# A hybrid decoder step on one core: the first loads regrouped, half of the first row scaling on GpSimd, and the first transposes woven into the first product

## The chip, the cores and the metric

The kernel runs on one core of one Trainium2 chip. The metric is device time in microseconds; the median of the runs counts. Engines are named as in the profile: PE (TensorE matmul), PEld (its weight load), DVE (VectorE), ACT (ScalarE), POOL (GpSimd) and SP (SyncE, which here only issues transfers).

## The reference, cut to what matters

One inference step of one decoder layer over 512 prompt rows and 32 sample rows of 1024 numbers each. The part that the change touches is the very beginning: the row normalisation of x and the first columns of the input projection.

```python
h = x * rsqrt(mean(x * x, axis=-1) + EPS) * norm_mix_pre     # 544 rows of 1024
proj = h @ w_in                                              # 1024 x 4608, cut into x_r | q | k | v | g
# attention bias: rel_bias[bucket(distance)], a table of 32 x 8
# then: causal conv and RG-LRU, windowed attention, gates, w_out, RMSNorm,
# ConvFFN (w_up 1024 x 8192, depthwise conv, gelu(gate) * value, w_down), RMSNorm
```

## The kernel before, in words

All products are made from float32 numbers that are split into a high part (rounded to the fast matmul type) and a low part (the rest): a product of a weight tile and an activation tile is three matmuls, high x high, high x low and low x high. Activations are kept with features on partitions (`h`, tiles hH and hL, eight of each for the eight 128-wide blocks k of the 1024 features), rows along the free dimension in two halves: half 0 is rows 0 to 255, half 1 the other 288.

The weights come 128 output columns at a time, 512 KB each: `wload` (L254) issues the load on SP into one of five `raw` buffers; `wsplit_hi` (L277) makes the two high halves on ACT and `wsplit_lo` (L282) the two low halves on DVE. `order` lists the column tiles as they are used; the first is called w0 below, the next w1, and so on. `mmhalf` (L165 is the matmul inside) issues the 24 matmuls of one column tile and one half; `step` gives them a PSUM buffer, and its tick then records the vector work that is due.

PE's, DVE's and ACT's instructions are kept in the order in which the code records them. POOL's and SP's order is made by a scheduler from the dependences it sees, so it need not be the order of the lines.

The start goes as follows. SP issues four loads of 256 KB for the first 256 rows (`xload(0)`, `xload(1)`; each row tile in two column halves z), a small one for the first norm weights, w0 and w1, then the other rows (`xload(2)` to `xload(4)`) and w2 to w4. POOL's own queue carries five small loads: the table `c_ohp` (L377), `rel_bias` into `relx` (L375) and three groups of norm weights into `rows_a` (L379); behind them stand, from a later line, a memset of the tile `lt` (L535), four loads of `rel_bias` into `rel` (L538), and sixteen small copies from `rel` to `lt` (L559). PE runs 18 warming matmuls on constants.

`xsquares` (L407 on ACT for the left column half, L409 on DVE for the right) sums the squares of a row tile; `xrstd` adds the two sums and makes the reciprocal root (a square root on ACT, then a reciprocal and one refining step on DVE). `xscale` multiplies the four half tiles: one on ACT, behind the two high splits of w0, and three on DVE. Then PE transposes the eight blocks (`ps_ta`, L448, two transposes of 128 x 128 for each), and `hsplit` makes hH on ACT (L433) and hL on DVE (L177 with tile hL) from each block. The first product (column tile w0, half 0, PSUM tile `pmin`) comes behind all sixteen transposes, in the order high x high, low weight x high, high x low, eight matmuls each. The next product (w1, half 0) follows, then a small product `ps_ohp` of `relx` and `ohp`, then w2.

Of the kernel before, what the change touches and what calls it, by code (L numbers as in the profile page):

```python
# [11 lines left out]
F32 = mybir.dt.float32  # L12
F32R = mybir.dt.float32r
AF = mybir.ActivationFunctionType
ALU = mybir.AluOpType
AX = mybir.AxisListType

P = 128
D = 1024
KD = D // P  # L20
# [9 lines left out]
NH = 8  # L30
NKV = 2
HD = 128
WIN = 128
NBK = 32
# [4 lines left out]
EPS = 1e-6  # L39
# [84 lines left out]
def hawk_step(ctx, tc, I, O):  # L124
    nc = tc.nc
    act, dve, pool, pe = nc.scalar, nc.vector, nc.gpsimd, nc.tensor
# [13 lines left out]
    cp = mixer.enter_context(tc.tile_pool(name="mixer_const", bufs=1))  # L140
    mixer.enter_context(tc.manual_schedule(engines={act.engine, dve.engine}))

    def S(name, dt=F32):
        return sp.tile([P, SLOT], dt, tag="s", name=name)

    def T(name, dt=F32):
        return tp.tile([P, FLAT + 4], dt, tag="t", name=name)
# [4 lines left out]
    def PM(name):  # L152
        return psm.tile([P, 512], F32, tag="mm", name=name)

    def PX(name):
        return psx.tile([P, 512], F32, tag="aux", name=name)
# [4 lines left out]
    def f32(ap):  # L161
        return ap.bitcast(F32)

    def mm(out, l, r, start, stop):
        pe.matmul(out, l, r, start=start, stop=stop)  # L165
# [4 lines left out]
    def mul(out, a, b):  # L170
        dve.tensor_tensor(out=out, in0=a, in1=b, op=ALU.mult)

    def add(out, a, b):
        dve.tensor_tensor(out=out, in0=a, in1=b, op=ALU.add)  # L174

    def stt(out, a, s_, b, op0, op1):
        dve.scalar_tensor_tensor(out=out, in0=a, scalar=s_, in1=b, op0=op0, op1=op1)  # L177
# [9 lines left out]
    def sides():  # L187
        for e in sorted((e for e in side if e[0] <= now[0]), key=lambda e: e[:2]):
            try:
                e[0] = now[0] + (next(e[2]) or 1)  # L190
            except StopIteration:
                side.remove(e)

    def tick(target=0, dt=1):
        now[0] += dt
        todo = late[:]
        late.clear()
        split = [wsplit_hi(u) for u in wclaim(target)]
        sides()
        for f in todo:  # L200
            f()
        for u in split:
            wsplit_lo(*u)
        for f in last:
            f()
        last.clear()
# [6 lines left out]
    ident = keep.tile([P, P], F32, name="ident")  # L213
# [9 lines left out]
    def wsrc(key):  # L223
        kind = key[0]
        if kind in ("wr", "wi"):
            return I["lru_" + kind][0, 4 * key[1]:4 * key[1] + 4].rearrange("n c d -> c n d")
        w = {"in": w_in, "lo": I["w_lru_o"][0], "ao": I["w_attn_o"][0], "out": I["w_out"][0]}[kind]
        c = key[-1]
        return w[:, c * P:(c + 1) * P].rearrange("(k p) n -> p k n", p=P)

    qkv_order = (16, 18, 8, 9, 10, 11, 17, 19, 12, 13, 14, 15)
    order = [("in", c) for c in qkv_order]
# [6 lines left out]
    wpos = {k: i for i, k in enumerate(order)}  # L239
    in_slots = {("out", c) for c in range(3, 8)} | {("in", c) for c in qkv_order[3:FIRST]}  # L240
    wraw, wunits, wnext = {}, {}, [0]

    def wname(i):
        return "_".join(str(z) for z in order[i])

    def wload(i):
        key = order[i]
        raw = wraw[i] = rp.tile([P, KD, P], F32, tag="raw", name="raw_" + wname(i))
        if key[0] == "wg":
            for z, nme in enumerate(("lru_wr", "lru_wi")):  # L250
                nc.sync.dma_start(out=raw[:, 4 * z:4 * z + 4, :],
                                  in_=I[nme][0, 4 * key[1]:4 * key[1] + 4].rearrange("n c d -> c n d"))
        else:
            nc.sync.dma_start(out=raw, in_=wsrc(key))  # L254
# [26 lines left out]
    def wsplit_lo(raw, hl, eng=None):  # L281
        (eng or dve).tensor_tensor(out=hl[1], in0=raw, in1=f32(hl[0]), op=ALU.subtract)  # L282

    def upto(key, a, look):
        return 2 * (wpos[key] + look) + a + 1
# [28 lines left out]

    def mmhalf(ps, key, X, a, ks=range(KD)):
        n = X.half[a][1] - X.half[a][0]
        if key == order[0] and a == 0:

            for j, (i0, i1) in enumerate(((0, 0), (1, 0), (0, 1))):
                for k in ks:  # L320
                    mm(ps[:, :n], wunits[2 * wpos[key] + k // 4][i0][:, k % 4, :], X.get(k, a, i1),
                       j == 0 and k == 0, j == 2 and k == KD - 1)
            return
        for k in ks:
            wh, wl = (wunits[2 * wpos[key] + k // 4][j][:, k % 4, :] for j in range(2))
            xh, xl = X.get(k, a, 0), X.get(k, a, 1)
            mm(ps[:, :n], wh, xh, k == 0, False)
            mm(ps[:, :n], wh, xl, False, False)
            mm(ps[:, :n], wl, xh, False, k == KD - 1)

    def step(key, X, a, done, target=None, look=2, quick=False):


        ps = PM("pm" + "_".join(str(z) for z in key) + f"_{a}")
        if quick:
            mmhalf(ps, key, X, a, range(4))
            now[0] += 0.5
            sides()
            mmhalf(ps, key, X, a, range(4, 8))
            done(a, ps)  # L340
        else:
            mmhalf(ps, key, X, a)
        tick(upto(key, a, look) if target is None else target, 0.5 if quick else 1)
        if not quick:
            late.append(lambda: done(a, ps))
# [6 lines left out]
    rows_a = cp.tile([32, P], F32, name="rows_a")  # L352
    warm = keep.tile([P, 1], F32, name="warm")
    act.activation(warm, epst, AF.Sqrt)
    xt = {}

    def xload(i):
        t0, n, src = TOK[i]
        for z in range(2):
            xt[i, z] = S(f"x{i}_{z}")  # L360
            nc.sync.dma_start(out=xt[i, z][:n, 0:512], in_=src[:, 512 * z:512 * z + 512])

    xload(0)
    xload(1)
    nc.sync.dma_start(out=rows_a[0:8, :], in_=I["norm_mix_pre"].rearrange("o (k p) -> (o k) p", p=P))
# [2 lines left out]
    xload(2)  # L368
    xload(3)
    xload(4)  # L370
    for i in (2, 3, 4):
        wload(i)
    relx = cp.tile([NBK + 1, NH], F32, name="relx")
    pool.memset(relx, 1.0)
    pool.dma_start(out=relx[0:NBK, :], in_=I["rel_bias"])  # L375
    ohp = T("ohp")[:NBK + 1, 0:3 * WIN]
    pool.dma_start(out=ohp, in_=I["c_ohp"])  # L377
    for r, nme in ((8, "norm_mix_post"), (16, "norm_ffn_pre"), (24, "norm_ffn_post")):
        pool.dma_start(out=rows_a[r:r + 8, :], in_=I[nme].rearrange("o (k p) -> (o k) p", p=P))  # L379
    pv = keep.tile([P, 96], F32, name="pv")  # L380

    pw = PX("ps_warm")
    ps0 = PX("ps_rows_a0")
# [5 lines left out]
    def newton_rstd(r, v, s_, sq):  # L389

        act.activation(s_, sq, AF.Sqrt, scale=1.0 / D, bias=epst)
        dve.tensor_scalar(v, sq, 1.0 / D, EPS, ALU.mult, ALU.add)
        dve.reciprocal(r, s_)
        mul(s_, r, r)
        stt(s_, s_, -0.5, v, ALU.mult, ALU.mult)
        stt(r, s_, 1.5, r, ALU.add, ALU.mult)

    h = Full("h")
    for k in range(KD):
        h.alloc(k)  # L400
    ss = cp.tile([P, 4, 5], F32, name="ss")
    dve.memset(ss, 1.0)

    def xsquares(i):
        n = TOK[i][1]
        jk, jv = T(f"jk{i}"), T(f"jv{i}")
        act.activation(jk[:n, 0:512], xt[i, 0][:n, 0:512], AF.Square, accum_out=ss[:n, 0, i:i + 1])  # L407
        xb = xt[i, 1][:n, 0:512]
        dve.scalar_tensor_tensor(out=jv[:n, 0:512], in0=xb, scalar=1.0, in1=xb, op0=ALU.mult, op1=ALU.mult,  # L409
                                 accum_out=ss[:n, 1, i:i + 1])  # L410

    def xrstd(lo, hi):
        c = slice(lo, hi)
        add(ss[:, 0, c], ss[:, 0, c], ss[:, 1, c])
        newton_rstd(ss[:, 1, c], ss[:, 3, c], ss[:, 2, c], ss[:, 0, c])

    def xscale(i, engines):
        n = TOK[i][1]
        r = ss[:n, 1, i:i + 1]
        for z in range(2):  # L420
            x_ = xt[i, z][:n, 0:512]
            if engines[z] == "a":
                act.activation(x_, x_, AF.Copy, scale=r)
            else:
                dve.tensor_scalar(x_, x_, r, None, ALU.mult)

    def xtile(i, k):
        n = TOK[i][1]
        return xt[i, k // 4][:n, (k % 4) * P:(k % 4 + 1) * P]

    def hsplit(k, a, ps):
        g = pv[:, G_PRE + k:G_PRE + k + 1]
        act.activation(h.get(k, a, 0), ps, AF.Copy, scale=g)  # L433
        stt(h.get(k, a, 1), ps, g, f32(h.get(k, a, 0)), ALU.mult, ALU.subtract)

    xsquares(0)
    xsquares(1)
    xrstd(0, 2)
    split = [wsplit_hi(u) for u in wclaim(2)]
    xscale(0, "av")  # L440
    xscale(1, "vv")
    dve.tensor_copy(pv[:, 0:8], ps0[:, 0:8])
    for u in split:
        wsplit_lo(*u)
    for k in range(KD):
        ps = (PM if k in (5, 6) else PX)(f"ps_ta{k}")
        for i in range(2):
            pe.transpose(ps[:, i * P:(i + 1) * P], xtile(i, k), ident)  # L448
        hsplit(k, 0, ps[:, :256])

    def norm_b():
        last.extend(lambda i=i: xsquares(i) for i in (2, 3, 4))
# [1182 lines left out]
    for i, x in enumerate(plan):  # L1635
# [7 lines left out]
        else:  # L1643
            _, q, c, a = x
# [113 lines left out]
    for i in range(2):  # L1758
        for kk in range(2):
            ps = tokens(i, kk)  # L1760
# [13 lines left out]
    r = rstd(1)  # L1774
# [36 lines left out]
```

## Time and profile before

| | |
|---|---|
| runs | 1006.45, 1008.0 and 1010.39 us |
| median | 1008.0 us |
| the profiled execution | span 1006.6 us (from its first to its last instruction; no other time is given for it) |
| granted TensorE clock over the span | 0.996 of full |
| busy: PE, DVE, ACT, POOL | 98%, 73%, 58%, 15% of the span |

The profile is of one execution. All times inside it are counted from the start of its span. A row of the timeline gives start, duration, engine, line, operation, output and inputs, a count where rows were merged, and in brackets how long the engine had been idle and what ended that. A row of the windows gives, for a stretch of time, the busy time of each engine, the granted clock, the busy share of the transfer engines and what they moved.

### The profile page before, as it was taken

The numbers are of one execution on the slowest core, as the hardware profiler recorded it, in microseconds if no ns is written. First come the engines' busy times: TensorE is split into PE (matmuls) and PEld (weight loads), VectorE is DVE, ScalarE is ACT, GpSimd is POOL, SyncE is SP. The second block draws the span as 40 slices with busy tenths as digits, with TensorE's granted clock in tenths as the row PEclk, the third lists the DMA queues.
The fourth block names the chain that finished last, engine by engine and source line by source line (L and its number), as shares of the span: only waits on it lengthen the run. The fifth ranks groups of instructions, "written<-read, shape, count | busy, mean of one in ns | idle before, by whom it ended". The sixth has DMA issues, their size and how long they took to land.

```text
span 1006.6 us, 20151 instructions
## 1 busy us (share of the span) xinstructions
PE 991.0 (98%) x7819; PEld 980.2 (97%) x7819; DVE 731.3 (73%) x1552; ACT 579.9 (58%) x1421; POOL 150.5 (15%) x270
## 2 busy tenths in 40 slices
PE   7999999999999999999999999999999999999997
PEld 7999999999999999999999999999999999999995
DVE  6476688545935655489777788888888888878865
ACT  6444454468458534556776656565656555555652
POOL 3131010001404432120001111111111101110003
PEclk9999999999999999999999999999999999999999
DMA  7743222323322344417245858586867676776612
GB/s 209 231 145 97 63 80 85 110 88 90 97 84 85 105 137 133 120 53 222 71 111 127 193 123 192 125 191 126 189 134 181 145 170 153 162 169 157 215 45 90
DMA packets 207687, 133.40 MB, mean 133 GB/s; under 512 B 6546, under 2 KB 194306, under 8 KB 207560
## 3 DMA queue, kind: packets, MB, share of 16 engines
q1 hardware_dynamic: 197944, 112.20, 39.2%
q0 software_dynamic: 9600, 17.90, 11.2%
q10 hardware_dynamic: 48, 2.03, 0.5%
q8 instruction: 61, 1.00, 0.4%
q14 instruction: 34, 0.28, 0.1%
HBM read 111.82 MB, written 9.14 MB: 120 GB/s over the span
## 4 chain that ended last, share of the span: by engine, by line
PE 93%; DVE 2%; DMA 2%; ACT 1%; issue 0%; SPq 0%; DVEq 0%
PE pmin L165 22%; PE pmdn L165 17%; PE pux L1396 15%; PE puy L1396 7%; PE pq L1396 6%; PE pmout L165 5%; PE pmao L165 5%; PE pmlo L165 4%; PE puz L1396 4%; PE pg L165 1%; PE psc L165 1%; PE ptok L165 1%; PE pvp L165 1%; DMA raw_up_s<-in_w_up_dram 1%; DMA raw_in<-in_w_in_dram 1%; PE pt L701 1%
## 5 line engine op out<-in xcount | busy, mean ns | idle before, releaser
L165 PE MATMUL pmin<-hH,wh_in 128*128 128x256 f32 (+1 forms) x576 | 167.1, 292 | 0.0
L165 PE MATMUL pmin<-hH,wl_in 128*128 128x256 f32 (+1 forms) x576 | 164.8, 288 | 0.0
L165 PE MATMUL pmin<-hL,wh_in 128*128 128x256 f32 (+1 forms) x576 | 164.7, 288 | 0.0
L165 PE MATMUL pmdn<-fH,wh_dn 128*128 128x256 f32 (+1 forms) x448 | 129.3, 289 | 0.2 <-DVE ft L174 0.2
L165 PE MATMUL pmdn<-fH,wl_dn 128*128 128x256 f32 (+1 forms) x448 | 129.3, 289 | 0.2 <-DVE wl_dn L168 0.2
L165 PE MATMUL pmdn<-fL,wh_dn 128*128 128x256 f32 (+1 forms) x448 | 129.2, 288 | 0.0
L177 DVE SCALAR_TENSOR_TENSOR uc<-u,fv,uc 128x560 f32<-128x560 f32 x128 | 101.9, 796 | 13.3 <-ACT uc L1427 13.2
L165 PEld LDWEIGHTS pmin<-hH,wh_in 128*128 128x128 f32 x576 | 108.3, 189 | 1.5 <-issue 0.6
L165 PEld LDWEIGHTS pmin<-hL,wh_in 128*128 128x128 f32 x576 | 108.2, 189 | 0.0
L165 PEld LDWEIGHTS pmin<-hH,wl_in 128*128 128x128 f32 x576 | 107.9, 188 | 0.0
L165 PEld LDWEIGHTS pmdn<-fH,wh_dn 128*128 128x128 f32 x448 | 84.4, 188 | 0.6 <-issue 0.6
L165 PEld LDWEIGHTS pmdn<-fH,wl_dn 128*128 128x128 f32 x448 | 84.5, 189 | 0.4 <-DVE wl_dn L168 0.4
L165 PEld LDWEIGHTS pmdn<-fL,wh_dn 128*128 128x128 f32 x448 | 84.3, 188 | 0.0
L1522 ACT COPY u<-pux 128x272 f32<-128x272 f32 x52 | 20.1, 386 | 85.9 <-PE pux L1396 85.9
L168 DVE TENSOR_TENSOR u<-puy,u 128x240 f32<-128x240 f32 (+2 forms) x78 | 24.6, 344 | 50.1 <-PE puy L1396 32.5
L174 DVE TENSOR_TENSOR ft<-ft,pmdn 128x256 f32<-128x256 f32 (+1 forms) x104 | 45.2, 435 | 16.2 <-PE pmdn L165 15.9
L277 ACT ACTIVATE wh_in<-raw_in 128x512 fp32r<-128x512 f32 x72 | 44.2, 628 | 20.8 <-PE pmin L165 10.4
L282 DVE TENSOR_TENSOR wl_in<-raw_in,wh_in 128x512 fp32r<-128x512 f32 x72 | 48.2, 683 | 1.6 <-ACT wh_in L277 1.5
L1427 ACT ACTIVATE uc<-u,fv 128x560 f32<-128x560 f32 x64 | 48.2, 754 | 0.0
L664 ACT ACTIVATE s<-s,st 128x256 f32<-128x256 f32 (+1 forms) x32 | 15.2, 475 | 50.7 <-DVE st L661 43.3
L168 DVE TENSOR_TENSOR wl_dn<-raw_dn,wh_dn 128x512 fp32r<-128x512 f32 x56 | 38.3, 685 | 0.0
L1322 POOL DMA_DIRECT2D raw_up_s<-raw_up_s x26 | 22.7, 872 | 101.7 <-issue 5.0
(758 smaller groups left out, 3406.3 us busy)
## 6 DMA issues: line engine op xcount, KB each, us to landing
raw_in<-in_w_in_dram SPq DMA_DIRECT2D x36, 512.0 KB
raw_dn<-in_w_down_dram SPq DMA_DIRECT2D x56, 256.0 KB
raw_up_s<-in_w_up_dram SPq DMA_DIRECT2D x26, 512.0 KB
raw_up_s<-raw_up_s POOLq DMA_DIRECT2D x26, 256.0 KB, 5.8
raw_ao<-in_w_attn_o_dram SPq DMA_DIRECT2D x8, 512.0 KB
raw_lo<-in_w_lru_o_dram SPq DMA_DIRECT2D x8, 512.0 KB
raw_out<-in_w_out_dram SPq DMA_DIRECT2D x8, 512.0 KB
x1d<-x SPq DMA_DIRECT2D x8, 272.0 KB
```

Of the source, the lines that this page charges most:

```text
L165: pe.matmul(out, l, r, start=start, stop=stop)
L168: dve.tensor_tensor(out=out, in0=a, in1=b, op=ALU.subtract)
L174: dve.tensor_tensor(out=out, in0=a, in1=b, op=ALU.add)
L177: dve.scalar_tensor_tensor(out=out, in0=a, scalar=s_, in1=b, op0=op0, op1=op1)
L277: act.activation(hl[0], raw, AF.Copy)
L282: (eng or dve).tensor_tensor(out=hl[1], in0=raw, in1=f32(hl[0]), op=ALU.subtract)
L664: act.activation(s3[:, j, :], s3[:, j, :], AF.Exp, bias=ng[:, j:j + 1], accum_out=sm[:, j:j + 1])
L701: pe.transpose(pt[:, (2 * ch + j) * P:(2 * ch + j + 1) * P], s3[:, j, ch * P:(ch + 1) * P], ident)
L1322: pool.dma_start(out=w["p4"], in_=w["p2"], accum_op=ALU.add)
L1396: pe.matmul(ps[:, :HN], w, x, start=start and k == 0 and i == 0, stop=stop and k == 3 and i == 2, skip_group_check=True)
L1427: act.activation(yt[j][:, 0:FLATU], u[:, 0:FLATU], AF.Copy, scale=fv[:, j:j + 1])
L1522: act.copy(e[nm_], z)
```

## The change

- The five small loads leave POOL's queue. They are issued by SP, behind the row tiles and w2 and ahead of w3 and w4.
- The sum of squares is finished otherwise: POOL makes `vsum` from ACT's sums, DVE adds its own sums to that in one instruction, and the square root reads the result.
- Of the four half tiles that are scaled, DVE takes three and POOL one (row tile 1, right half). ACT takes none.
- The two low halves of w0 are made on POOL.
- The first product gets its PSUM buffer (`pm_first`) before the transposes, and its matmuls stand between them: high x high two blocks behind the transposes, high x low three blocks behind, and the eight low weight x high ones last.

In the built program everything else stands as before on each engine. On POOL the scheduler places the new instructions behind what was there: memset `relx`, memset `lt`, the four loads of `rel`, the sixteen copies to `lt`, then `vsum`, the first low half of w0, the scaling, the second low half of w0.

```diff
@@ mmhalf, step @@
-        if key == order[0] and a == 0:
-
-            for j, (i0, i1) in enumerate(((0, 0), (1, 0), (0, 1))):
-                for k in ks:
-                    mm(ps[:, :n], wunits[2 * wpos[key] + k // 4][i0][:, k % 4, :], X.get(k, a, i1),
-                       j == 0 and k == 0, j == 2 and k == KD - 1)
-            return
...
-        ps = PM("pm" + "_".join(str(z) for z in key) + f"_{a}")
-        if quick:
+        first_ = key == order[0] and a == 0
+        ps = first_ps if first_ else PM("pm" + "_".join(str(z) for z in key) + f"_{a}")
+        if first_:
+            pass
+        elif quick:
@@ loads @@
-    for i in (2, 3, 4):
-        wload(i)
-    relx = cp.tile([NBK + 1, NH], F32, name="relx")
-    pool.memset(relx, 1.0)
-    pool.dma_start(out=relx[0:NBK, :], in_=I["rel_bias"])
-    ohp = T("ohp")[:NBK + 1, 0:3 * WIN]
-    pool.dma_start(out=ohp, in_=I["c_ohp"])
+    wload(2)
+    nc.sync.dma_start(out=relx[0:NBK, :], in_=I["rel_bias"])
+    nc.sync.dma_start(out=ohp, in_=I["c_ohp"])
     for r, nme in ((8, "norm_mix_post"), (16, "norm_ffn_pre"), (24, "norm_ffn_post")):
-        pool.dma_start(out=rows_a[r:r + 8, :], in_=I[nme].rearrange("o (k p) -> (o k) p", p=P))
+        nc.sync.dma_start(out=rows_a[r:r + 8, :], in_=I[nme].rearrange("o (k p) -> (o k) p", p=P))
+    wload(3)
+    wload(4)
@@ start @@
-    xrstd(0, 2)
+    pool.tensor_scalar(vsum, ss[:, 0, 0:2], 1.0 / D, EPS, ALU.mult, ALU.add)
+    r_, s_, v_ = (ss[:, z, 0:2] for z in (1, 2, 3))
+    stt(v_, ss[:, 1, 0:2], 1.0 / D, vsum, ALU.mult, ALU.add)
+    act.activation(s_, v_, AF.Sqrt)
+    dve.reciprocal(r_, s_)
+    mul(s_, r_, r_)
+    stt(s_, s_, -0.5, v_, ALU.mult, ALU.mult)
+    stt(r_, s_, 1.5, r_, ALU.add, ALU.mult)
     split = [wsplit_hi(u) for u in wclaim(2)]
-    xscale(0, "av")
-    xscale(1, "vv")
-    dve.tensor_copy(pv[:, 0:8], ps0[:, 0:8])
+
+    def scale0(eng, i, z):
+        eng.tensor_scalar(xt[i, z][:, 0:512], xt[i, z][:, 0:512], ss[:, 1, i:i + 1], None, ALU.mult)
+
+    scale0(dve, 0, 0)
+    scale0(pool, 1, 1)
+    scale0(dve, 1, 0)
+    scale0(dve, 0, 1)
     for u in split:
-        wsplit_lo(*u)
+        wsplit_lo(*u, eng=pool)
+    first_ps = PM("pm_first")
+
+    def first_mm(k, i0, i1, start=False, stop=False):
+        mm(first_ps[:, :256], wunits[k // 4][i0][:, k % 4, :], h.get(k, 0, i1), start, stop)
+
-    for k in range(KD):
-        ps = (PM if k in (5, 6) else PX)(f"ps_ta{k}")
-        for i in range(2):
-            pe.transpose(ps[:, i * P:(i + 1) * P], xtile(i, k), ident)
-        hsplit(k, 0, ps[:, :256])
+    for k in range(KD + 3):
+        if k < KD:
+            ps = (PM if k in (5, 6) else PX)(f"ps_ta{k}")
+            for i in range(2):
+                pe.transpose(ps[:, i * P:(i + 1) * P], xtile(i, k), ident)
+            if k == 0:
+                dve.tensor_copy(pv[:, 0:8], ps0[:, 0:8])
+            hsplit(k, 0, ps[:, :256])
+        if 0 <= k - 2 < KD:
+            first_mm(k - 2, 0, 0, start=k == 2)
+        if 0 <= k - 3 < KD:
+            first_mm(k - 3, 0, 1)
+    for k in range(KD):
+        first_mm(k, 1, 0, stop=k == KD - 1)
```

More of the change, by code (lines that the diff above doesn't have):

```diff
@@ L361, in xload @@
             nc.sync.dma_start(out=xt[i, z][:n, 0:512], in_=src[:, 512 * z:512 * z + 512])
+    relx = cp.tile([NBK + 1, NH], F32, name="relx")
+    pool.memset(relx, 1.0)
+    ohp = T("ohp")[:NBK + 1, 0:3 * WIN]
     xload(0)
@@ L434, in hsplit @@
         stt(h.get(k, a, 1), ps, g, f32(h.get(k, a, 0)), ALU.mult, ALU.subtract)
+    vsum = cp.tile([P, 2], F32, name="vsum")
     xsquares(0)
     xsquares(1)
-    xrstd(0, 2)
-    split = [wsplit_hi(u) for u in wclaim(2)]
-    xscale(0, "av")
-    xscale(1, "vv")
-    dve.tensor_copy(pv[:, 0:8], ps0[:, 0:8])
-    for u in split:
-        wsplit_lo(*u)
+    pool.tensor_scalar(vsum, ss[:, 0, 0:2], 1.0 / D, EPS, ALU.mult, ALU.add)
[6 more added lines that the diff above has]
+    stt(r_, s_, 1.5, r_, ALU.add, ALU.mult)
+    split = [wsplit_hi(u) for u in wclaim(2)]
+    def scale0(eng, i, z):
[4 more added lines that the diff above has]
+    scale0(dve, 0, 1)
+    for u in split:
+        wsplit_lo(*u, eng=pool)
[14 more added lines that the diff above has]
+            first_mm(k - 3, 0, 1)
     for k in range(KD):
-        ps = (PM if k in (5, 6) else PX)(f"ps_ta{k}")
-        for i in range(2):
-            pe.transpose(ps[:, i * P:(i + 1) * P], xtile(i, k), ident)
-        hsplit(k, 0, ps[:, :256])
+        first_mm(k, 1, 0, stop=k == KD - 1)
     def norm_b():
```

## The prediction, made blind

> **What bounds the kernel now.** I read the page first: its span and, by engine, the chain that ended last.
>
> ```profile
> span 1006.6 us, 20151 instructions
> PE 93%; DVE 2%; DMA 2%; ACT 1%; issue 0%; SPq 0%; DVEq 0%
> ```
>
> The kernel is a queue of matmuls. A change at the start can only bring forward or put back the moment from which PE runs without a gap. Nothing behind that moment changes its order, so the shift is carried to the end: the span changes by as much as the end of the first product does. The chain in order of time shows what leads there (start, duration).
>
> ```profile
> 9.80 1.15 ACT wh_in L277 x2
> 10.95 0.62 ACT x L423
> ...
> 11.62 3.51 PE ps_ta L448 x16
> 15.13 5.77 PE pmin L165 x48
> 20.90 0.74 PE ps_ohp L165 x2
> ```
>
> PE's transposes wait until 11.62, because ACT scales its quarter of the rows behind the two high splits of w0. From there PE is busy throughout. The timeline gives the end of the first product, which is the start of the next one:
>
> ```profile
> 16.95 1.11 PE L165 MATMUL pmin<-hL,wh_in 128*128 128x256 f32 x8
> 17.91 0.28 PE L165 MATMUL pmin<-hH,wh_in 128*128 128x256 f32 x1
> ```
>
> So the whole change plays before 17.91. Call the new value F; the forecast is F minus 17.91. Eight matmuls took 0.96 us here, 0.12 each. The windows (stretch, its length, busy PE, PEld, DVE, ACT, POOL, then granted clock) show that they were slower earlier:
>
> ```profile
> 5.01:8.42 3.41, 2.64 (x23) 2.36 (x21) 1.04 (x4) 0.72 (x2) 1.50 (x4) 1.00 0.90 259
> 8.42:11.83 3.41, 0.21 (x2) 0.21 (x3) 3.06 (x12) 2.06 (x4) 0.00 (x0) 1.00 1.13 333
> 11.83:15.25 3.42, 3.42 (x18) 3.42 (x17) 3.04 (x7) 3.07 (x8) 2.54 (x16) 0.50 1.14 265
> 15.25:18.66 3.41, 3.41 (x31) 3.41 (x31) 3.38 (x10) 3.41 (x10) 0.00 (x0) 1.00 1.18 283
> ```
>
> PE stood idle from 8.42 nearly to 11.83, then had half the clock for 3.42 us, and the full one from 15.25. Sixteen transposes took 3.51 at half clock: 0.22 each, so I take 0.11 at the full one and 0.23 for a slow matmul.
>
> **Moving the five small loads.** POOL issues them before the loads of `rel`; behind stand the sixteen copies.
>
> ```profile
> 1.57 0.73 POOL L377 DMA_DIRECT2D ohp<-in_c_ohp_dram  x1
> ...
> 4.36 0.22 POOL L535 MEMSET lt<- 128x128 f32 x1
> 4.51 1.50 POOL L538 DMA_DIRECT2D rel<-in_rel_bias_dram  x3
> ...
> 11.88 2.67 POOL L559 COPY lt<-rel 32x8 f32<-32x8 f32 x16 [4.72 <-DMA rel<-in_rel_bias_dram]
> ```
>
> Today these copies delay nobody. In the built order of the changed kernel `vsum` stands behind them, and the whole normalisation waits for `vsum`. This is the step that I expect to decide. Without the five loads the `rel` loads are issued at about 1.65, 2.15, 2.65 and 3.15 (from 1.57 the memset of `lt` comes first; 0.50 each). Landing times from issue, in the view of transfers:
>
> ```profile
> ohp<-in_c_ohp_dram POOLq DMA_DIRECT2D x1, 49.5 KB, 4.8
> ...
> relx<-in_rel_bias_dram POOLq DMA_DIRECT2D x1, 1.0 KB, 4.3
> ...
> rows_a<-in_norm_mix_post_dram POOLq DMA_DIRECT2D x1, 4.0 KB, 5.2
> rows_a<-in_norm_ffn_pre_dram POOLq DMA_DIRECT2D x1, 4.0 KB, 6.3
> ```
>
> The fourth lands 4.3 to 6.3 after 3.15; I take 4.8, the middle of the first three issued (those quoted with 4.8, 4.3 and 5.2), so 8.0. Its last four copies cost 0.67 (a quarter of 2.67), and `vsum` 0.3, as other small ones (count, busy, mean ns, idle):
>
> ```profile
> L517 POOL TENSOR_SCALAR cc<-cc 128x8 f32<-128x8 f32 x7 | 2.1, 305 | 0.6
> ```
>
> So `vsum` is there at v = 8.9 (bounds 8.4 and 10.4). Before, the sums were joined at 8.44:
>
> ```profile
> 7.64 0.69 DVE L409 SCALAR_TENSOR_TENSOR jv<-x 128x512 f32<-128x512 f32 x1 [2.29 <-DMA x<-in_x_prompt_dram]
> ...
> 8.44 0.16 DVE L174 TENSOR_TENSOR ss<-ss 128x2 f32<-128x2 f32 x1
> ...
> 8.64 0.29 ACT L391 ACTIVATE ss<-ss,epst 128x2 f32<-128x2 f32 x1 [0.96 <-DVE ss L174]
> ...
> 9.75 1.28 DVE L425 TENSOR_SCALAR x<-x,ss 128x512 f32<-128x512 f32 x3
> ...
> 12.69 3.47 DVE L177 SCALAR_TENSOR_TENSOR hL<-ps_ta,pv,hH 128x256 fp32r<-128x256 f32 x8 [0.39 <-ACT hH L433]
> ```
>
> The second row tile may land earlier without the loads that compete with it, by 0 to 0.8 us (the time of 256 KB at the 333 GB/s of a window above; I allow 0.5). With `vsum` at 8.9 that is worth nothing. On SP the five loads cost some 2 us of issue and put back w3 and w4, not w0 to w2, nor the row tiles. `ps_ohp`, which reads `relx` and `ohp`, stands at 20.90, and w3 is used behind it, so I cost this at nothing. Without that cover PE would stall for as long as the later load is late.
>
> **The new sum.** One instruction and `vsum` replace the join and the side product; the chain from join to first scaling stays 1.3 (8.44 to 9.75). ACT's square root starts 0.2 after the join and ends 0.3 later, then the first high split takes 0.6, so w0's first high half is ready at v + 1.1.
>
> **GpSimd's two kinds of work.** What ACT and DVE are spared lies off the new path. What POOL gets is priced by rows of the recurrence, where it worked beside DVE:
>
> ```profile
> 322.94 2.52 DVE L883 TENSOR_TENSOR_SCAN hs<-rg,xc 128x568 f32<-128x568 f32 x1 [1.57 <-POOL xc L880]
> ...
> 326.92 1.33 DVE L883 TENSOR_TENSOR_SCAN hs<-rg,xc 128x568 f32<-128x568 f32 x1
> ```
>
> ```profile
> 322.86 1.40 POOL L877 TENSOR_TENSOR xc<-xc,lt 128x568 f32<-128x568 f32 x1
> ```
>
> POOL's two-input instruction took 1.40 for 568 columns, so 1.26 for the 512 of a low half. POOL's first low half is queued ahead of its scaling and runs from v + 1.1 to v + 2.4, just when DVE is to start scaling at v + 1.3. The scan took 1.33 alone and 2.52 when POOL had started 0.08 earlier: DVE waited almost the whole of POOL's instruction. If scaling waits likewise, it starts at v + 2.4. DVE needs 0.9 for the two tiles that the first transposes want (three took 1.28), and POOL's own scaling, at most 1.26 and at least 0.3, becomes ready at the same moment; I charge half of about 1.0. PE then starts at v + 3.8 = 12.7. Unblocked it would be v + 2.2 = 11.1, so the term is bounded by 0 and 2.1 us. No row shows a one-input DVE instruction beside POOL. The Trainium skill, "Advanced Engine Details and Errata", section "VectorE Performance Modes", says that the second SBUF port of VectorE is shared and that GpSimd and two-port VectorE instructions block each other. By it a scaling in that mode is blocked as the scan was, which gives 12.7; without it 11.1.
>
> POOL's scaled tile is wanted by the fifth pair of transposes, over 2 us after the first; its second low half by the end. Both are in time.
>
> **The interleaving.** PE has the same sixteen transposes and 24 matmuls. At half clock a block costs 0.44 for its transposes and 0.46 for two matmuls, so the transposes come every 0.9 us instead of 0.44. DVE takes 0.43 a block (eight hL in 3.47), so it now waits for PE, and ACT with it. From PE's start to the first hL 1.07 passed (11.62 to 12.69), 0.63 of it behind the first pair. With PE's start at 12.7: three pairs until 14.0, a matmul and a pair until 14.7, two matmuls until 15.1, then full clock. The last four pairs at 0.22, with the two matmuls between them at 0.23, end at about 16.75. The last hL starts 0.63 later, ends at 17.85, and behind it stand one high x low and eight low matmuls, 1.05: F = 18.9. By PE's work alone it would be 18.5. So F - 17.91 = +1.0. From an equal start the interleaving would itself cost about 0.4, as the transposes come later and the low weights stay behind the last hL. Bounds: +0.1 (unblocked) and +2.1 (v at 10.4, clock as here).
>
> The Trainium skill, "TensorE: Matmul & The Clock Gate", section "Part 4: PE-mode transpose", states that transposes do not count as PE activity for the full clock. This trace differs: a window with hardly anything but transposes was followed by 1.00 at 15.25. By the page the clock would come back one window later, as in the third rival below.
>
> On the profiled execution the sum is 1006.6 + 1.0 = 1007.6; that execution lies 1.4 under the median of 1008.0, so the predicted median is 1009.0. A measurement of this kernel tells about 0.5%, 5 us, from no change; the three runs alone lie 3.9 apart.
>
> **The rivals.** First, it does what the edits suggest: `rel` lands before 6.6, POOL is free in time, the second row tile lands 0.5 earlier, and DVE isn't blocked. The join is at 7.95, PE starts at 10.2, the last hL ends near 15.6 and F is 16.6, or 15.6 if the shorter idle time keeps the full clock. That is -1.3 to -2.3; I take -1.5, 1006.5. For it speaks the early issue; against it all landings of 4.3 and more.
>
> Second, the copies gate but DVE isn't blocked: +0.1, 1008.1. For it: DVE's copy-like instructions were never seen blocked; against it the scan.
>
> Third, the clock. PE idles longer, and from 11.83 to 15.25 it would be busy 2.5 of 3.4 us. A window with 2.64 (from 5.01) kept the full clock, one with 0.21 lost it. If 2.5 isn't enough, half clock holds to 18.66: of 9.0 us of slow work (sixteen at 0.22, 24 at 0.23) 6.0 is done by then, the rest takes 1.5: F = 20.2, +2.3, 1010.3.
>
> Fourth, clearly slower: the `rel` loads land no earlier than today, as transfers of the row tiles and w0 hold them up and not their issue. The copies end at 14.55, v is 14.85, PE starts at 18.65 and F is 24.9, or 23.2 at full clock: +5.3 to +7.0, about 1014. The point from which this decides: every microsecond of the fourth landing past 8.0 costs one, and past 12 the loss is over 0.5%. Against it: the earlier issued loads landed earlier.
>
> **How the numbers follow.** Forecast 0.45; as intended 0.25; unblocked 0.17; clock 0.07; late `rel` 0.06. The range takes in all but the last: 1006.5 to 1010.3, widened by 0.7 and 1.0 for the scatter of the runs: 1005.8 to 1011.3. Faster by over 0.5% needs 5 us out of 17.91, of which 7 are loading: 0.02, for the scatter. Slower by over 0.5%: the fourth rival and a little scatter, 0.07. Within: 0.91.
>
> **What would show it.** Right: POOL's `lt` copies end near 8.6 and DVE's join starts behind `vsum` near 8.9; DVE's first scaling starts with the end of POOL's first low half; the transposes start near 12.7; the product of w1 starts near 18.9. Wrong: the join is released by DVE's own squares, or the first scaling starts 1.3 after it while POOL is busy, or the transposes start before 11.6.

## The result, and the profile after

The changed kernel takes 1011.7 us (median of 11 runs, 1010.3 to 1013.7) against 1008.3 us for the kernel before (11 runs beside them, 1006.5 to 1010.8). The ratio is 1.0033, 95% interval 1.0023 to 1.0043: slower by 0.33%, some 3.4 us. The forecast was 1009.0, with a range from 1005.8 to 1011.3. The profiled execution of the changed kernel took 1010.7 us, 1008.9 of it span.

The chain of waits of the changed kernel, in order of time (start, duration, what):

```profile
2.80 4.56 DMA rel<-in_rel_bias_dram
...
9.04 0.55 POOL lt L583 x4
...
9.68 0.19 POOL vsum L436
...
9.89 0.17 DVE ss L177
...
10.92 1.27 DVE ss L177
...
12.21 1.33 DVE x L447 x2
...
13.58 1.33 PE ps_ta L464 x5
```

Read it from the top: a load of 1 KB into `rel` (the third of four), the copies that wait for these loads, `vsum` queued behind them, and only then the normalisation of the rows. In the kernel before this chain began with w0 and passed through ACT; nothing of POOL was on it.

POOL's timeline (start, duration, line, operation, shapes, count, idle time before and what ended it):

```profile
5.78 1.19 POOL L583 COPY lt<-rel 32x8 f32<-32x8 f32 x8 [1.97 <-DMA rel<-in_rel_bias_dram]
7.41 0.57 POOL L583 COPY lt<-rel 32x8 f32<-32x8 f32 x4 [0.44 <-DMA rel<-in_rel_bias_dram]
9.01 0.57 POOL L583 COPY lt<-rel 32x8 f32<-32x8 f32 x4 [1.03 <-DMA rel<-in_rel_bias_dram]
9.68 0.18 POOL L436 TENSOR_SCALAR vsum<-ss 128x2 f32<-128x2 f32 x1
10.90 1.26 POOL L282 TENSOR_TENSOR wl_in<-raw_in,wh_in 128x512 fp32r<-128x512 f32 x1 [1.03 <-ACT wh_in L277]
12.28 2.10 POOL L447 TENSOR_SCALAR x<-x,ss 128x512 f32<-128x512 f32 x1
14.36 1.27 POOL L282 TENSOR_TENSOR wl_in<-raw_in,wh_in 128x512 fp32r<-128x512 f32 x1
```

The last four copies stood 1.03 us waiting for the fourth `rel` load. DVE's timeline beside it:

```profile
6.86 0.69 DVE L406 SCALAR_TENSOR_TENSOR jv<-x 128x512 f32<-128x512 f32 x1 [1.57 <-DMA x<-in_x_prompt_dram]
...
9.89 0.16 DVE L177 SCALAR_TENSOR_TENSOR ss<-ss,vsum 128x2 f32<-128x2 f32 x1 [2.33 <-POOL vsum L436]
...
10.72 1.45 DVE L177 SCALAR_TENSOR_TENSOR ss<-ss 128x2 f32<-128x2 f32 x2
12.21 1.71 DVE L447 TENSOR_SCALAR x<-x,ss 128x512 f32<-128x512 f32 x3
```

DVE had its own squares at 7.56 and stood idle for 2.33 us until `vsum`. Two instructions on 128 x 2 elements, 0.36 us together in the kernel before, took 1.45: the second ended at 12.19, just behind POOL's first low half (10.90 to 12.16).

PE, and the windows (stretch, its length, busy PE, PEld, DVE, ACT, POOL, granted clock):

```profile
12.75 0.47 PE L464 MATMUL ps_ta<-ident,x 128*128 128x128 f32 x1 [5.39 <-DVE x L447]
13.58 1.33 PE L464 MATMUL ps_ta<-ident,x 128*128 128x128 f32 x5 [0.36 <-DVE x L447]
...
20.89 0.28 PE L165 MATMUL pmin<-hH,wh_in 128*128 128x256 f32 x1
```

```profile
7.80:11.22 3.42, 0.00 (x0) 0.00 (x0) 0.95 (x5) 1.13 (x3) 1.26 (x8) 1.00 1.14 338
11.22:14.63 3.41, 1.52 (x7) 1.12 (x7) 2.77 (x6) 0.65 (x3) 3.29 (x3) 0.50 1.14 256
14.63:18.04 3.41, 3.41 (x18) 3.41 (x17) 2.44 (x6) 2.22 (x5) 1.00 (x1) 0.50 0.85 227
```

PE idled 5.39 us instead of 3.49, and the half clock lasted two windows, 11.22 to 18.04, instead of one. The product of w1 starts at 20.89: F moved by +2.98 us. From the start of the transposes (13.58, as the first came alone at 12.75; 11.62 before) to F it is 7.31 us instead of 6.29. So 1.96 us of the loss lie ahead of the transposes and 1.02 behind their start.

Behind F the matmuls follow in the same order in both kernels, but the shift isn't carried unchanged. Matmul by matmul it is 2.98 us at F, 2.57 at 200 us and 2.34 at 370 us, in steps of at most 0.1 us whose cause stays open. Then it falls by 1.0 at one wait, that for the second copy of the rows:

```profile
PE pxx L1024 <- DMA xx<-in_x_prompt_dram: 0.3, 1, 0.3
```

The first number is the whole wait; it was 1.3 us in the profile of before. It can't be put down to the change: with before's order and 32 warming matmuls it was short too, with moved loads alone it was long. The last matmul is 1.37 us late; the spans of the two profiled executions differ by 2.3, so 0.9 of that comes behind it.

### The profile page after: what moved, and what is told of

It reads as the page before. It is cut to its first block, busy times and chain, and to the rows that moved or that the text cites. A ratio compares the mean times of both kernels' runs of the same rounds, so it can differ in the third digit from the quotient of the medians.

```text
span 1008.9 us, 20149 instructions
## 1 busy us (share of the span) xinstructions
PE 991.8 (98%) x7819; PEld 980.0 (97%) x7819; DVE 732.8 (73%) x1549; ACT 579.9 (57%) x1420; POOL 151.6 (15%) x269
## 4 chain that ended last, share of the span: by engine, by line
PE 92%; DVE 3%; DMA 2%; ACT 2%; issue 1%; POOL 0%; DVEq 0%; POOLq 0%; SPq 0%; ACTq 0%
PE pmin L165 21%; PE pmdn L165 17%; PE pux L1420 15%; PE puy L1420 7%; PE pq L1420 6%; PE pmout L165 5%; PE pmao L165 5%; PE pmlo L165 4%; PE puz L1420 4%; PE pg L165 1%; PE psc L165 1%; PE pvp L165 1%; DMA raw_up_s<-in_w_up_dram 1%; PE pt L725 1%; PE ptok L165 1%
## 5 line engine op out<-in xcount | busy, mean ns | idle before, releaser
L165 PE MATMUL pmlo<-lH,wh_lo 128*128 128x272 f32 x128 | 37.8, 295 | 0.0
```

## The experiments

F is the number to compare, read from one profile of each; the ratio to the kernel before, with its interval, comes from 7 to 12 runs of the kernel against 27 to 32 of the kernel before (11 and 11 for the changed kernel). The fourth column counts from the first transpose, or from the second where the first came alone (12.75 and 13.58 above).

| kernel | F | F - 17.91 | transposes to F | half clock there | ratio |
|---|---|---|---|---|---|
| after | 20.89 | +2.98 | 7.31 | 11.22 to 18.04 | 1.0033 (1.0023 to 1.0043) |
| after, `vsum` on DVE | 19.32 | +1.41 | - | 10.33 to 17.16 | 1.0008 (0.9995 to 1.0020) |
| after, low halves on DVE | 21.39 | +3.48 | 8.90 | 12.25 to 19.08 | 1.0037 (1.0022 to 1.0052) |
| after, 36 warming matmuls | 19.16 | +1.25 | 5.78 | none | 1.0005 (0.9994 to 1.0016) |
| after, no interleaving | 19.29 | +1.38 | 6.02 | 12.47 to 15.88 | 1.0033 (1.0020 to 1.0046) |
| after, no interleaving, 36 warming | 19.00 | +1.09 | 5.68 | none | 1.0012 (1.0002 to 1.0022) |
| after, `vsum` on DVE, 36 warming | 17.30 | -0.61 | 5.94 | none | 0.9999 (0.9988 to 1.0011) |
| before, loads moved | 17.04 | -0.87 | 6.29 | 10.99 to 14.41 | 0.9982 (0.9971 to 0.9993) |
| before, 32 warming | 17.69 | -0.22 | 5.67 | none | 0.9994 (0.9983 to 1.0006) |
| before, loads moved, 28 warming | 16.35 | -1.56 | 5.67 | none | 0.9983 (0.9972 to 0.9994) |
| the same, interleaved | 16.53 | -1.38 | 5.57 | none | 0.9991 (0.9979 to 1.0004) |
| the same, low halves on POOL, not interleaved | 17.23 | -0.68 | 5.66 | none | 0.9984 (0.9975 to 0.9993) |

**The queue.** The changed kernel with the side sum back on DVE:

```diff
-    pool.tensor_scalar(vsum, ss[:, 0, 0:2], 1.0 / D, EPS, ALU.mult, ALU.add)
+    dve.tensor_scalar(vsum, ss[:, 0, 0:2], 1.0 / D, EPS, ALU.mult, ALU.add)
```

> The changed kernel with vsum made on DVE, not on POOL. Theory 'queue' (vsum stands behind the copies to lt): the sums are joined at about 7.9 instead of 9.9, the first scaling starts near 9.0 while POOL is still copying, the transposes start near 10 instead of 13.6 and the product of w1 starts at 17 to 18 instead of 20.9; the time is about 3 us under the changed kernel, near 1008.5. Rival 'port alone' (DVE would wait for POOL's first low half in any case): the transposes start no earlier than 12.5 and the time stays above 1010.5.

DVE's, POOL's and ACT's timelines of that kernel:

```profile
8.21 0.16 DVE L436 TENSOR_SCALAR vsum<-ss 128x2 f32<-128x2 f32 x1
...
9.26 0.36 DVE L177 SCALAR_TENSOR_TENSOR ss<-ss 128x2 f32<-128x2 f32 x2
9.65 2.29 DVE L447 TENSOR_SCALAR x<-x,ss 128x512 f32<-128x512 f32 x3
```

```profile
9.36 0.85 POOL L583 COPY lt<-rel 32x8 f32<-32x8 f32 x4 [0.65 <-DMA rel<-in_rel_bias_dram]
10.29 1.37 POOL L282 TENSOR_TENSOR wl_in<-raw_in,wh_in 128x512 fp32r<-128x512 f32 x1
```

```profile
12.11 1.20 ACT L430 ACTIVATE hH<-ps_ta,pv 128x256 fp32r<-128x256 f32 x3 [1.56 <-DVE pv L466]
```

`vsum` follows DVE's own squares at once, although the row tile landed later in this profile (the squares began at 7.59, at 6.86 above). The refinement is undisturbed (0.36). The copies still end after 10.2, and nobody waits for them. F is 1.57 us earlier, at 19.32 and not at the 17 to 18 that were expected. The transposes do start near 10, at 10.19, but hH waits until 12.11 for the small copy to `pv`, which stands on DVE behind the scalings (so the table has no figure from the transposes on). What is left of the loss: POOL's low half now meets the scaling (three half tiles in 2.29 instead of 1.28), and the half clock still runs for two windows.

**Who holds DVE.** The changed kernel with w0's low halves back on DVE:

```diff
     for u in split:
-        wsplit_lo(*u, eng=pool)
+        wsplit_lo(*u)
```

> The changed kernel with both low halves of w0 on DVE, not on POOL. Theory 'port' (DVE's refining step and first scaling wait for POOL's low half): vsum stays near 9.9, the refining step ends near 11.2 instead of 12.2, the transposes start at 12.2 to 12.6 instead of 13.6; the low halves now stand before hL on DVE, so the product of w1 starts near 20, 1 us earlier, and the time is about 1010.7. Rival 'no port': the transposes stay at 13.6 and the extra 1.3 us on DVE makes the time 1012 or more.

DVE, POOL and ACT of that kernel:

```profile
10.72 0.36 DVE L177 SCALAR_TENSOR_TENSOR ss<-ss 128x2 f32<-128x2 f32 x2
11.12 1.72 DVE L447 TENSOR_SCALAR x<-x,ss 128x512 f32<-128x512 f32 x3
12.75 1.28 DVE L282 TENSOR_TENSOR wl_in<-raw_in,wh_in 128x512 fp32r<-128x512 f32 x2
13.96 0.15 DVE L466 COPY pv<-ps_rows_a 128x8 f32<-128x8 f32 x1
```

```profile
11.18 2.12 POOL L447 TENSOR_SCALAR x<-x,ss 128x512 f32<-128x512 f32 x1 [1.32 <-DVE ss L177]
```

```profile
14.20 1.21 ACT L430 ACTIVATE hH<-ps_ta,pv 128x256 fp32r<-128x256 f32 x3 [2.87 <-DVE pv L466]
```

The refinement falls back from 1.45 to 0.36 us with the same start, 10.72, so POOL's low half was what held it. The Trainium skill, "Advanced Engine Details and Errata", section "VectorE Performance Modes", states that the second SBUF port of VectorE is shared, and that GpSimd and two-port VectorE instructions block each other. The trace agrees as far as POOL's instruction held one of DVE, here one on two columns; whether that one uses two ports no run shows.

The time did not fall (1.0037 against 1.0033). The transposes came 1.1 us earlier (11.66, then 12.49), but the two low halves then stood on DVE ahead of the small copy to `pv`, without which ACT can't make hH: hH started at 14.20 instead of 14.10. One wait took the place of another. Moving the low halves to POOL cost DVE 1.1 us at the refinement and spared it 1.28 ahead of `pv`. F is 0.50 later, more than the 0.10 of hH; the rest stands beside a half clock that ended at 19.08 here and at 18.04 in the changed kernel.

**The clock.** The changed kernel with `WARM = 36` in place of 18, which keeps PE busy until 11.5:

> The changed kernel with 36 warming matmuls instead of 18, so that PE is busy until about 11. Theory 'clock' (PE idles over 6 us, so that the transposes and most of the first product run at half clock): the granted clock stays 1.00 through the transposes, these start at 13.6 as before, the product of w1 starts near 19.3 instead of 20.9, the time falls by 1.5 to 2.5 to about 1009.5. Rival 'clock doesn't matter' (ACT and DVE set the pace of the blocks): the product of w1 starts at 20.5 to 21 and the time stays at 1011.7.

The first two rows are PE's timeline, the others the windows of that kernel:

```profile
12.55 0.33 PE L464 MATMUL ps_ta<-ident,x 128*128 128x128 f32 x1 [0.84 <-DVE x L447]
13.38 0.77 PE L464 MATMUL ps_ta<-ident,x 128*128 128x128 f32 x5 [0.50 <-DVE x L447]
```

```profile
8.64:12.05 3.41, 3.06 (x28) 2.85 (x26) 1.96 (x6) 1.24 (x3) 2.03 (x6) 1.00 1.10 357
12.05:15.47 3.42, 2.15 (x14) 1.73 (x15) 2.82 (x7) 1.59 (x4) 3.36 (x2) 1.00 1.08 223
```

The transposes start at nearly the same time, and F is 1.73 us earlier. The ratio falls from 1.0033 to 1.0005. On the kernel before, the same cure is worth less: `WARM = 32` there,

> The kernel before with 32 instead of 18 warming matmuls and nothing else. Clock theory: the half-clock window 11.83 to 15.25 goes, the transposes start as before near 11.6 but at full speed, the eight hL (0.43 us each) become the pace, and the product of w1 starts at about 17.2 instead of 17.91: -0.7 us, ratio 0.9993. Rival, the clock hardly matters here since DVE's hL set the pace anyway: the product of w1 stays at 17.7 to 17.9, ratio 1.000. In the changed kernel the same edit was worth 1.75 us, since it took away two half-clock windows and not one.

gave 5.67 us instead of 6.29 from the first transpose to F, 0.62. Its F is nevertheless 17.69 and not the expected 17.2, since w0 landed later in that execution (the high split began at 10.21, at 9.80 in the profile of before). The ratio, 0.9994 (0.9983 to 1.0006), can't be told from 1.

**The loads alone.** The kernel before with nothing but the five small loads moved to SP, behind w2:

```diff
-    for i in (2, 3, 4):
-        wload(i)
-    pool.dma_start(out=relx[0:NBK, :], in_=I["rel_bias"])
...
+    wload(2)
+    nc.sync.dma_start(out=relx[0:NBK, :], in_=I["rel_bias"])
...
+    wload(3)
+    wload(4)
```

> The kernel before with only the five small loads moved to SP, behind w2. Theory 'loads help': the second row tile is read at about 6.2 and 6.9 instead of 6.95 and 7.64, w0 is there near 9.1 instead of 9.8, the transposes start near 11.0 instead of 11.6, and the product of w1 starts 0.6 earlier with the same clock; the time is about 0.6 under the kernel before, 1007.7. Rival 'SP late': the five issues on SP put back w3 and w4 or ps_ohp so that PE waits between 20 and 30, and the time is over 1009.

DVE, ACT and PE of that kernel:

```profile
6.88 0.69 DVE L411 SCALAR_TENSOR_TENSOR jv<-x 128x512 f32<-128x512 f32 x1 [1.81 <-DMA x<-in_x_prompt_dram]
```

```profile
8.94 1.15 ACT L277 ACTIVATE wh_in<-raw_in 128x512 fp32r<-128x512 f32 x2 [0.72 <-DMA raw_in<-in_w_in_dram]
```

```profile
10.75 3.49 PE L450 MATMUL ps_ta<-ident,x 128*128 128x128 f32 x16 [1.95 <-ACT x L425]
...
17.04 0.28 PE L165 MATMUL pmin<-hH,wh_in 128*128 128x256 f32 x1
```

The second row tile and w0 both land about 0.8 us earlier (7.64 and 9.80 before), and all behind follows: F -0.87. The ratio's interval lies wholly below 1 and takes in the 0.9991 that 0.87 us would give. The size rests on one pair of profiles: where w0 was waited for, its split began between 8.86 and 9.76 in six kernels with moved loads, and at 9.80 and 10.21 in two without. So one of the changed kernel's five edits is a gain, and the others give away 3.9 us of F.

With 28 warming matmuls in addition:

> The kernel before with the five small loads on SP behind w2 and 28 warming matmuls. If the two gains add up: transposes at 10.75 as with the loads alone, clock 1.00 throughout, product of w1 at about 16.4 (17.04 with the loads alone), -1.5 us against the kernel before, ratio 0.9985 or, with what the loads alone measured, 0.9976. If the clock is worth nothing there: 17.0, ratio 0.9982 as with the loads alone.

F is 16.35, as the sum of the two has it; aligned by PE's instructions, this execution runs 1.56 us ahead of the profile of before from F to 370 us without a change. The ratio, 0.9983, is that of the loads alone, so the clock's 0.6 us can't be seen in the times, only in the profile.

**The interleaving.** Taken out of the changed kernel: the sixteen transposes first, then high x high, low weights, high x low.

```diff
-    for k in range(KD + 3):
-        if k < KD:
...
-        if 0 <= k - 2 < KD:
-            first_mm(k - 2, 0, 0, start=k == 2)
-        if 0 <= k - 3 < KD:
-            first_mm(k - 3, 0, 1)
-    for k in range(KD):
-        first_mm(k, 1, 0, stop=k == KD - 1)
+    for k in range(KD):
...
+    for k in range(KD):
+        first_mm(k, 0, 0, start=k == 0)
+    for k in range(KD):
+        first_mm(k, 1, 0)
+    for k in range(KD):
+        first_mm(k, 0, 1, stop=k == KD - 1)
```

> The changed kernel with its interleaving taken out: the sixteen transposes first, then the product in the old order (high x high, low weights, high x low). Loads, GpSimd's vsum, scaling and low halves stay. The first transpose should stay at 12.75 and the half clock should again run from about 11.2 to 18.0. If interleaving costs at half clock (the transposes, and with them DVE's hL, come at a block's pace of 0.86 us): hL ends near 17.9 and the start of the product of w1 comes about 0.5 us earlier than in the changed kernel, 20.4 instead of 20.89; against the kernel before +2.5 us, time ratio 1.003. If interleaving helps (it fills PE while hL is made): the start of that product comes at 21.4 or later, 0.5 us or more later than in the changed kernel.

Its windows:

```profile
9.05:12.47 3.42, 0.04 (x1) 0.04 (x1) 2.49 (x7) 1.24 (x3) 2.17 (x5) 1.00 1.09 358
12.47:15.88 3.41, 3.05 (x13) 2.76 (x14) 2.80 (x7) 2.10 (x5) 2.85 (x2) 0.50 1.04 223
15.88:19.29 3.41, 3.41 (x29) 3.25 (x28) 3.41 (x8) 3.41 (x11) 0.00 (x0) 1.00 1.10 293
```

The half-clock window, 12.47 to 15.88, held nothing but transposes (the first matmul of the product starts at 16.13), 3.05 us of them, and the full clock followed: here transposes did bring it back.

F is 19.29, but this profile caught the windows in another place and lost one half-clock window, not two, so its F doesn't compare with 20.89; and the time is the changed kernel's, 1.0033. This run alone left it undecided. At one clock, with 36 warming matmuls in both:

> The changed kernel without its interleaving (as in the run without interleaving) and with 36 warming matmuls, so that it meets the changed kernel with 36 warming matmuls at the same clock of 1.00; there the product of w1 started 5.76 us after the second transpose (13.38 to 19.14). If interleaving with the low weights last costs at any clock (hL at the pace of the blocks, eight low matmuls behind the last hL): 5.1 us or less behind the second transpose, product of w1 near 18.4, time 0.6 us below that kernel. If the cost exists only at half clock: 5.6 to 5.8, the same product near 19.0, the same time.

From the second transpose to F it is 5.68 us without and 5.78 with interleaving. Of the two expectations the 5.1 was wrong and the 5.6 to 5.8 right: high x high isn't free behind the transposes but follows hH (eight matmuls from 15.06 to 17.13), and PE's order makes little of it either way. The ratios (1.0012 and 1.0005, from two sets of runs) don't tell the two apart. At full clock the interleaving is worth nothing measurable; what it costs at half clock no pair of runs shows.

A better mix, put on the good version (moved loads, 28 warming matmuls), with the low weights inside the blocks:

> As the kernel with moved loads and 28 warming matmuls, and in addition transposes and first product are interleaved with the low weights inside the blocks (block k: transposes of k, high x high and low x high of k-2, high x low of k-3); low halves and all scaling stay where the kernel before has them. If interleaving pays once PE runs at full clock: hL ends near 15.4 as without it, only one matmul or two stand behind it, and the product of w1 starts at 15.8, about 0.6 us earlier than without interleaving; -2.1 us against the kernel before, ratio 0.998 to 0.997. Rival, interleaving costs at any clock since the transposes come later: 16.6 or later.

From the first transpose to F it is 5.57 instead of 5.67, and F itself, 16.53 where 15.8 was expected, is later than 16.35 because the transposes began 0.28 later. What follows is worse. PE of that kernel, and ACT:

```profile
24.26 1.96 PE L470 MATMUL ps_tb<-ident,x 128*128 128x128 f32 x10 [0.28 <-ACT x L421]
```

```profile
13.53 2.21 ACT L431 ACTIVATE hH<-ps_ta,pv 128x256 fp32r<-128x256 f32 x4 [0.33 <-PE ps_ta L452]
15.63 1.14 ACT L277 ACTIVATE wh_in<-raw_in 128x512 fp32r<-128x512 f32 x2
```

ACT's eight hH end at 15.7, 1.6 us later than in the kernel without interleaving (14.2), as the transposes come at the blocks' pace. ACT's queue behind them, w1's and w2's splits and the normalisation of the other rows, is late by as much; the second batch of transposes begins at 23.71 instead of 22.95 and waits, behind its first, until 24.26. By 27 us PE is some 1.25 us behind, of which the start explains 0.28. The gain at F is paid back with interest by the engine that the transposes feed.

**Both at once, and the low halves on POOL behind its copies.** The changed kernel with `vsum` on DVE and 36 warming matmuls:

> The changed kernel with vsum on DVE and 36 warming matmuls: the queue and the clock are taken away together, GpSimd's low halves, its scaling and the interleaving stay. With vsum on DVE alone hH began at 12.11 and the product of w1 at 19.3 with the half clock until 17.16. If the two add up: hL from about 12.4 at 0.45 each, one matmul and eight low matmuls behind it, product of w1 at 17.1, -0.8 us against the kernel before, ratio 0.9992. If a third thing of the same size is at work (GpSimd holding DVE's scaling, the interleaving): 17.9 or later, ratio 1.000 or more.

F is 17.30, 0.61 ahead of before, where 17.1 was expected: the queue and the clock add up, and nothing of their size is left. The time is that of before, 0.9999. (In this kernel the warming matmuls themselves, until 11.2, held the transposes back to 11.36, 1.2 us later than with 18 of them.)

The version with moved loads and 28 warming matmuls, its two low halves on POOL:

> As the kernel with moved loads and 28 warming matmuls, with one more edit: the two low halves of w0 on GpSimd, where they stand behind the sixteen copies to lt and so behind DVE's scalings, not on DVE in front of its hL. If an instruction that reads PSUM is not held by GpSimd (in the changed kernel hL ran at 0.45 us beside GpSimd's second low half): hL from 11.2 instead of 12.01 and the product of w1 at about 15.7 instead of 16.35; -2.2 us against the kernel before, ratio 0.9978. If GpSimd holds hL as it held the refinement of the reciprocal: hL from about 12.2, product of w1 at 16.4, ratio 0.9983 as without the edit.

Inconclusive. w0's split began at 9.76 in this profile, so the transposes came at 11.57 and F at 17.23; from the transposes it is 5.66, as without the edit. The ratio is 0.9984 (0.9975 to 0.9993).

The version that beats both kernels is thus the smallest: the kernel before with the five loads moved, 1007.8 us (0.9982), and with or without more warming matmuls it measures the same.

## Why the prediction was wrong, step by step

**Right in kind: the copies gate.** The join was released by `vsum`, and that the second row tile landed 0.78 earlier was worth nothing, since `vsum` came later still. With `vsum` taken out of the queue F fell by 1.57 us.

**The first step that failed: the fourth landing, 8.0.** It landed at 8.96. The forecast took 4.8 us from issue, the middle of three other loads of that queue; the view of the tile `rel` after:

```profile
L562 POOL DMA_DIRECT2D rel<-in_rel_bias_dram x4: 518/522/702, 1.6 to 3.3; - x4
...
DMA to landing us min/median/max: 4.0/4.3/5.7
```

The median, 4.3, is even below that value, but the last of four decides, and it took 5.7, within the stated 4.3 to 6.3. For a wait on several transfers the upper end was the one to take. `vsum` ended at 9.87 instead of 8.9: 0.97 us.

**Right: DVE is held.** First scaling at v + 2.34 (forecast v + 2.4), though the place was another: POOL's low half began at 10.90, 0.02 ahead of the refinement's second instruction, and held that. From there to the transposes 1.37 against 1.4: DVE's two scalings took 1.33 instead of 0.9 beside POOL's. POOL's own scaling, "about 1.0", took 2.10, but its tile was wanted late. In sum the transposes stood at v + 3.71 (forecast v + 3.8); only v was off.

**The second step that failed: the clock, "two matmuls until 15.1, then full clock".** This case was the third rival, at 0.07, with F at 20.2. Behind the transposes' start the forecast allowed 6.2 us; 7.31 came. With 36 warming matmuls it is 5.78, so 1.53 of the 7.31 are half clock. The rival asked whether a window with 2.5 us of PE would be enough; the window had only 1.52, because PE began later and because the windows don't start with the kernel. Rows of the runs, all on a kernel's own windows: at half clock, 1.52, 2.27 and 2.69 us of 3.41 didn't bring the clock back, 3.05 and 3.42 did; at full clock 1.77, 2.15 and 2.64 kept it, 1.46, 1.71 and less lost it. A chance of 0.07 was far too low: by these rows a window with 2.5 us, as the forecast had it, would not have brought the clock back either. The interleaving may have a part in this. The three half-clock windows that failed are those of interleaved kernels, in two of which PE waited 0.72 and 0.91 us for hH between the transposes; the three that brought the clock back are those of kernels without interleaving. Against it stands the time without interleaving, 1.0033 as with it. No pair of runs with the windows in the same place decides it.

The two steps account for the miss: 18.9 + 0.97 + 1.1 (7.31 less 6.2) is 20.97, and F is 20.89. In the time the forecast was 2.7 us short, 2.0 of them this F; the rest is the baseline (1008.3, not 1008.0) and what a single profiled execution doesn't tell. The forecast also assumed that the shift at F is carried to the end. In the one pair of profiles it was not (2.98 at F, 1.37 at the last matmul), so the time follows F only roughly.

**Half right: the loads, "worth nothing".** For the row tiles in the changed kernel, yes. Alone the move is worth 0.87 us of F, which the forecast never priced, as it counted only the row tiles and not w0, which also lands earlier. **Right: SP's side at nothing.** `ps_ohp` ran at 23.9 without a wait. **Off: the interleaving, put at about 0.4 from an equal start.** At full clock it was 0.10.

So F from before to after, each size from a pair of profiles above: 17.91; -0.62 without before's own half clock (17.29); -0.94 for the loads (16.35); +0.95 for POOL's scaling and low halves, the interleaving and the long warming together (17.30; 0.68 of it is the later start of the transposes, 11.36 for 10.68, and POOL's scaling was never run alone); +1.86 for `vsum` in POOL's queue (19.16); +1.73 for the half clock (20.89). The half clock isn't due to `vsum`'s wait alone: with `vsum` on DVE it still ran for two windows, 10.33 to 17.16.

## What to carry to other kernels

An instruction that finishes a critical value shouldn't stand on an in-order engine behind anything that waits for a transfer, however small: here 0.18 us of work cost 1.6 to 1.9 us of F. The half clock behind an idle stretch of the matmul engine cost as much again. Price an idle stretch of TensorE with the clock it costs, and take the slowest landing where several are waited for. Of a bundle of edits, run each alone: the gain of one hid under the losses of the rest.

## What was not expected of the hardware

The half clock also comes in mid-run, with PE busy throughout as the profile has it, in some executions and not in others. The windows of the changed kernel with 36 warming matmuls (the first and third rows are the windows in front):

```profile
199.80:203.20 3.40, 3.40 (x33) 2.82 (x32) 1.22 (x4) 1.03 (x5) 0.00 (x0) 1.00 0.15 43
203.20:206.60 3.40, 3.40 (x19) 3.40 (x18) 2.12 (x11) 0.89 (x6) 0.00 (x0) 0.50 0.53 155
216.80:220.27 3.47, 3.47 (x29) 3.18 (x28) 0.17 (x1) 0.21 (x2) 0.00 (x0) 1.00 0.50 151
220.27:223.70 3.43, 3.43 (x18) 3.43 (x17) 1.22 (x7) 1.99 (x10) 0.00 (x0) 0.50 0.53 158
```

Each costs 1.5 to 1.6 us (aligned by PE's instructions). The profiles of before and after had none; seven of the eleven experiments had one or two, all within 202 to 207 or 216 to 224 us. One such window takes 0.0017 off the mean clock (half of 3.41 in 1009), and the runs of the changed kernel sort by it: five at 0.992 and 0.993 took 1012.3 to 1013.7, six at 0.994 and 0.995 took 1010.3 to 1011.7. So these windows, and how many fall on the start, probably make much of the scatter of a few microseconds that both kernels show. What brings them on in mid-run stays open. That the windows run free of the kernel is what the Trainium skill states ("TensorE: Matmul & The Clock Gate", section "Part 1: The HAM clock gate (the "warmup" mystery)"); the trace agrees: here the first half-clock window began anywhere from 10.33 to 12.47 us in the six profiles that had one at the start.

POOL's one-input scaling of 128 x 512 took 2.10 us beside DVE's scaling, longer than a two-input low half of the same shape (1.26); after DVE's scaling was done, in the kernel with `vsum` on DVE and 36 warming matmuls, it took 1.58. hL, which reads PSUM, was hardly slowed beside POOL's second low half (three in 1.34, against 1.27 in the kernel with the low halves on DVE), unlike the refinement and the scaling, which read SBUF alone.
